# Scan of a hybrid decoder layer: scores and decays placed behind the new state, decays by one minimum and a biased exponential

## The chip, the cores and the metric

One core of one Trainium2 chip. The metric is the device time of one execution of the program in microseconds; it is given as the median of several runs. The engines are TensorE (PE, with its weight loads PEld), VectorE (DVE), ScalarE (ACT), GpSimd (POOL) and SyncE (SP), which here issues the DMA transfers.

## The reference

One decoder layer for a prompt of 1024 tokens and a batch of 8 samples of 4 tokens, width 1024, everything in float32: a SwiGLU block, a mixer, a second SwiGLU block, a gated embedding and a final norm. The change lies in the mixer's chunked scan (16 heads of 64 in 2 groups, state 128, chunks of 128 tokens):

```python
da = dt * a;  xdt = x * dt;  a_cum = cumsum(da)            # within a chunk
seg = a_cum[q] - a_cum[s]
decay_in = where(q >= s, exp(seg), 0)
scores = einsum('qn,sn->qs', C, B)
y_diag = einsum('qs,sp->qp', scores * decay_in, xdt)
decay_out = exp(a_cum[last] - a_cum)
chunk_states = einsum('sn,sp->pn', B, xdt * decay_out)
h = h_prev * exp(a_cum[last]) + chunk_states               # chunk after chunk
y_off = einsum('qn,pn->qp', C, h_prev) * exp(a_cum)
y = y_diag + y_off + d_skip * x
```

## The kernel before, in words

The scan works in 16 units: unit u is chunk u // 2 and head group u % 2 (8 heads). Products of 32-bit precision are made of rounded high and low parts: a tensor is copied to a rounded type on ScalarE (its name ends in h) and the rest is taken on VectorE (its name ends in l); a matmul of two such tensors is three matmuls.

For one unit the functions are called in this order.

- `scan_first` transposes the unit's inputs and B and makes the scores on TensorE, into the banks `btr` and `bsc`. VectorE makes `xd` (x times dt), `skip` writes d_skip times x to `xD`; GpSimd makes `xde`; ScalarE copies B to `bt`. VectorE masks the scores (`sm`) and multiplies the decays `Wa` with them (L1101). Then come parts of the unit before: `scan_lower` gives `wl`, the low part of its weights, and `scan_split` the two parts of its `xD`, `yoh` on ScalarE and `yol` on VectorE. The decays of unit u+1 are loaded by a DMA (`decay_load`, L993) to the half of `Wa` that `scan_lower` has just read for the last time. At the end the parts `xdh` and `xdl` of `xd` are taken.
- One chunk of an independent product (the rest of the input projection, then part of the output projection: 24 matmuls of L258) stands here in TensorE's order, with what the other engines do for it: a weight split now and then (L235, L236) and a copy or an addition of the result (L1214, L1231). In some units pool operands are split as well (L1197, L1198).
- `scan_state` multiplies C with the old state on TensorE; GpSimd decays the state, VectorE scales the result by `eA` to `yo` (written over `xd` here), GpSimd adds it to `xD`; TensorE makes the chunk's state, and VectorE adds it to `h`.
- `scan_last(u - 1)` makes the output of the unit before on TensorE: four groups of five matmuls, in the order yoh, yol, wh by xdh, wh by xdl, wl by xdh (L1158).
- `scan_mid` copies the finished weights of unit u to `wh` on ScalarE and makes the decays of unit u+1 (`decay`): on VectorE eight instructions, one for each head, that subtract a per-partition number from a row of sums and take the minimum with zero (L1000), then one exponential over all eight heads on ScalarE (L1001).
- `y_out(u - 1)` copies the output out of its banks with four copies on ScalarE (L1010) and stores it.
- After an odd unit a second product chunk follows.

The orders of TensorE, VectorE, ScalarE and GpSimd are the order of the program text here (`manual_schedule`); the order of SP's queue is left to the planner. Before the units, `scan_sample` runs for the two groups of the samples; it calls `decay` with 32 tokens. The sums that `decay` subtracts are in `ac`, made once in `steps2`.

Of the kernel before, what the change touches and what calls it, by code (L numbers as in the profile page):

```python
# [10 lines left out]
AF = mybir.ActivationFunctionType  # L11
ALU = mybir.AluOpType
# [3 lines left out]
P = 128  # L16
D = 1024
# [9 lines left out]
GH = 8  # L27
# [29 lines left out]
C_TRI = C_ID + P  # L57
# [26 lines left out]
def emit(tc, dr):  # L84
    nc = tc.nc
    V, S, G, PE, SY = nc.vector, nc.scalar, nc.gpsimd, nc.tensor, nc.sync
# [6 lines left out]
    def new(pool, name, n, dt=F32):  # L93
        uid[0] += 1
        return At(pool.tile([P, n], dt, name=f"{name}_{uid[0]}"))
# [11 lines left out]
    def phase(name, side="left"):  # L107
        return tc.alloc_tile_pool(name=name, bufs=1, side=side, reuse_waits="tile")

    def f(o, n, p0=0, p1=P):  # L110
        return o.f[p0:p1, o.c : o.c + n]

    def r(o, n, p0=0, p1=P):
        return o.t[p0:p1, o.c : o.c + n]

    def cst(o, n, p1=P):
        return f(o_cst + o, n, 0, p1)
# [652 lines left out]
    ph = phase("pooling")  # L770
# [78 lines left out]
    NDT = 9 * H  # L849
    ph_m = phase("mixer", "right")  # L850
    o_bc = new(ph_m, "bc", 4 * T)
    o_dtp, o_ac, o_eA, o_dO = (new(ph_m, f"dt{i}", NDT) for i in range(4))
    o_cd, o_cds = new(ph_m, "cd", P), new(ph_m, "cds", P)
    ph_c = phase("conv", "right")
    o_xb = [new(ph_c, "xb", XCB), new(ph_c, "xb", XCB)]
    o_cv = new(ph_c, "cv", XCB)
# [17 lines left out]
    ph = ph_c  # L874
# [33 lines left out]
    def steps2():  # L908

        da = f(o_e, NDT)  # L910
        PE.matmul(pa[:, 0:128], lhsT=cst(C_TRI, P), rhs=da[:, 0:128], start=True, stop=True)
        PE.matmul(pa[:, 256:384], lhsT=cst(C_ONE, P), rhs=da[:, 0:128], start=True, stop=True)
        PE.matmul(pb[0:S3, 0:H], lhsT=cst(C_TRIS, S3, TS), rhs=da[0:TS, 128:144], start=True, stop=True)
        PE.matmul(pb[0:S3, 32 : 32 + H], lhsT=cst(C_BLK, S3, TS), rhs=da[0:TS, 128:144], start=True, stop=True)
        PE.matmul(pb[:, 128:256], lhsT=cst(C_ONE, P, TS), rhs=f(o_u, NB * H, 0, TS), start=True, stop=True)
        ac, eA, dO = f(o_ac, NDT), f(o_eA, NDT), f(o_dO, NDT)
        G.memset(f(o_ac + 128, H), 0.0)
        G.memset(f(o_dO + 128, H), 0.0)
        V.tensor_copy(ac[:, 0:128], pa[:, 0:128])
        V.tensor_copy(ac[0:S3, 128:144], pb[0:S3, 0:H])  # L920
        V.tensor_tensor(dO[:, 0:128], pa[:, 256:384], ac[:, 0:128], op=ALU.subtract)
        V.tensor_tensor(dO[0:S3, 128:144], pb[0:S3, 32 : 32 + H], ac[0:S3, 128:144], op=ALU.subtract)
        S.activation(eA, ac, AF.Exp)
        S.activation(dO, dO, AF.Exp)
        S.activation(f(o_cd, P), pa[:, 256:384], AF.Exp)
        S.activation(f(o_cds, P), pb[:, 128:256], AF.Exp)
# [12 lines left out]
    for i in range(12):  # L939
# [26 lines left out]
        if i in (0, 2, 3):  # L966
            {0: steps1, 2: steps2, 3: steps3}[i]()
# [8 lines left out]

    ph = phase("scan", "right")
    o_Wa, o_xd, o_xde, o_bt, o_sm = (new(ph, n_, k) for n_, k in (("Wa", 2048), ("xd", 512), ("xde", 512), ("bt", P), ("sm", P)))
    o_h, o_xD2 = new(ph, "h", D), new(ph, "xD", 1024)
    o_xD = o_xD2  # L980
    o_Wh2, o_Wl2 = new(ph, "wh", 2048, F32R), new(ph, "wl", 2048, F32R)
    o_xdh2, o_xdl2 = new(ph, "xdh", 1024, F32R), new(ph, "xdl", 1024, F32R)
    o_yoh, o_yol = new(ph, "yoh", 512, F32R), new(ph, "yol", 512, F32R)
    byd2, btr, bsc, byo, byd = banks[3:8]

    def h3(a):
        return a.rearrange("p (h e) -> p h e", h=GH)

    def by_head(o, hh, nt, k):
        return f(o + hh, GH, 0, nt).unsqueeze(2).to_broadcast([nt, GH, k])  # L990

    def decay_load(o, nt, rows):
        SY.dma_start(h3(f(o, GH * nt, 0, nt)), rows.unsqueeze(0).to_broadcast([nt, GH, nt]))  # L993

    def decay(o, hh, nt):

        ab = f(o, GH * nt, 0, nt)
        ab3 = h3(ab)
        for h in range(GH):
            V.tensor_scalar(ab3[:, h, :], ab3[:, h, :], f(o_ac + hh + h, 1, 0, nt), 0.0, op0=ALU.subtract, op1=ALU.min)  # L1000
        S.activation(ab, ab, AF.Exp)  # L1001

    def y_out(g, t0, nt, yd):

# [8 lines left out]
    def skip(o_y, nt, hh, g):  # L1013

        V.tensor_tensor(h3(f(o_y, 512, 0, nt)), h3(btr[0:nt, :]),
                        vec(V_DSK + GH * g, GH)[0:nt, :].unsqueeze(2).to_broadcast([nt, GH, 64]), op=ALU.mult)
# [65 lines left out]
    def unit(u):  # L1082
        c, g = u // 2, u % 2
        return c, g, c * H + GH * g, c * P

    def scan_first(u):

        c, g, hh, t0 = unit(u)
        B, C = f(o_bc + (g * T + t0), P), f(o_bc + ((2 + g) * T + t0), P)
        for j in range(4):  # L1090
            PE.transpose(btr[:, j * P : j * P + P], f(o_xs + ((4 * g + j) * T + t0), P), ident)
        PE.transpose(bsc[:, 0:P], B, ident)
        PE.matmul(bsc[:, 128:256], lhsT=B, rhs=C, start=True, stop=True)
        bt, sm, xd, xde, ab = f(o_bt, P), f(o_sm, P), f(o_xd, 512), f(o_xde, 512), f(o_Wa + 1024 * (u % 2), 1024)
        ab3 = h3(ab)
        V.tensor_tensor(h3(xd), h3(btr[:, :]), by_head(o_dtp, hh, P, 64), op=ALU.mult)
        G.tensor_tensor(h3(xde), h3(xd), by_head(o_dO, hh, P, 64), op=ALU.mult)
        skip(o_xD2 + 512 * (u % 2), P, hh, g)
        S.copy(bt, bsc[:, 0:P])
        V.tensor_tensor(sm, bsc[:, 128:256], cst(C_TRI, P), op=ALU.mult)  # L1100
        V.tensor_tensor(ab3, ab3, sm.unsqueeze(1).to_broadcast([P, GH, P]), op=ALU.mult)  # L1101
        if u:
            scan_lower(u - 1)
            scan_split(u - 1)
        if u < 15:
            h1 = unit(u + 1)[2]
            decay_load(o_Wa + 1024 * ((u + 1) % 2), P, d_ac[h1 : h1 + GH, :])
        o_xh, o_xl = o_xdh2 + 512 * (u % 2), o_xdl2 + 512 * (u % 2)
        S.copy(r(o_xh, 512), xd)
        V.tensor_tensor(r(o_xl, 512), xd, f(o_xh, 512), op=ALU.subtract)  # L1110

    def scan_state(u):

        c, g, hh, t0 = unit(u)
        C = f(o_bc + ((2 + g) * T + t0), P)
        hg = f(o_h + 512 * g, 512)
        if c > 0:
            yo = f(o_xd, 512)
            PE.matmul(byo[:, :], lhsT=C, rhs=hg, start=True, stop=True)
            G.tensor_tensor(h3(hg), h3(hg), by_head(o_cd, hh, P, 64), op=ALU.mult)  # L1120
            V.tensor_tensor(h3(yo), h3(byo[:, :]), by_head(o_eA, hh, P, 64), op=ALU.mult)
            xD = f(o_xD2 + 512 * (u % 2), 512)
            G.tensor_tensor(xD, xD, yo, op=ALU.add)
        PE.matmul(btr[:, :], lhsT=f(o_bt, P), rhs=f(o_xde, 512), start=True, stop=True)
        if c > 0:
            V.tensor_tensor(hg, hg, btr[:, :], op=ALU.add)
        else:
            V.tensor_copy(hg, btr[:, :])
        if c == 7:
            SY.dma_start(dr["o_ssmp"][:, 512 * g : 512 * g + 512], hg)  # L1130

    def scan_split(u):

        xD = f(o_xD2 + 512 * (u % 2), 512)
        S.copy(r(o_yoh, 512), xD)
        V.tensor_tensor(r(o_yol, 512), xD, f(o_yoh, 512), op=ALU.subtract)

    def scan_mid(u):
        o_W, o_wh, o_wl = (o + 1024 * (u % 2) for o in (o_Wa, o_Wh2, o_Wl2))
        S.copy(r(o_wh, 1024), f(o_W, 1024))  # L1140
        if u < 15:
            decay(o_Wa + 1024 * ((u + 1) % 2), unit(u + 1)[2], P)

    def scan_lower(u):
        o_W, o_wh, o_wl = (o + 1024 * (u % 2) for o in (o_Wa, o_Wh2, o_Wl2))
        V.tensor_tensor(r(o_wl, 1024), f(o_W, 1024), f(o_wh, 1024), op=ALU.subtract)  # L1146
# [13 lines left out]
    def yout_args(u):  # L1160
        return u % 2, u // 2 * P, P, (byd, byd2)

    def scan():
        for g in range(2):
            yield from scan_sample(g)
        decay_load(o_Wa, P, d_ac[0:GH, :])
        decay(o_Wa, 0, P)
        yield
        for u in range(16):
            scan_first(u)  # L1170
            L.get("take", int)()
            yield
            scan_state(u)
            if u:
                scan_last(u - 1)
            scan_mid(u)
            if u:
                y_out(*yout_args(u - 1))
            L.get("take", int)()
            if u % 2:  # L1180
                yield
        scan_lower(15)
        scan_split(15)
        scan_last(15)
        y_out(*yout_args(15))
# [49 lines left out]
    def gated():  # L1235

        for c0, n in CH:
            for m in range(8):
# [11 lines left out]
                yield  # L1250

    a, b = scan(), products()
    done = object()
    with tc.manual_schedule(engines=MS):
# [8 lines left out]
    ph = phase("gated")  # L1263
# [23 lines left out]
    for m in range(8):  # L1287
# [3 lines left out]
        for k in range(4):  # L1291
            h, c, c0, n = k // 2, k % 2, CQ * k, CQ
# [208 lines left out]
```

## Time and profile before

| | us |
|---|---|
| median of 3 runs | 2313.32 (2313.03 to 2315.71) |
| the profiled execution | 2317.03 |
| its span | 2315.2 |
| the sixteen units, from the span's start | about 1074 to 1300 |

The profile is of one execution. PE is the matmuls and PEld their weight loads, which overlap them. In timelines each row is a run of equal instructions: its start, the time from the first start to the last end, engine, line, operation, output and inputs by the program's names, shapes and count; in brackets is the time that the engine sat idle ahead of it and what it waited for. `dt` is the name of the small tables (`ac` and its relatives), `W`, `X` and `tmp` belong to the product chunks. An instruction's record can begin before the record of the one ahead of it on its engine ends, so the distance of two starts is a little shorter than a duration.

### The profile page before, as it was taken

To read this page: it belongs to the slowest core of one execution; us is meant where nothing else is said; L and a number is where in the kernel's file an instruction comes from. 1 tells how busy PE (TensorE), PEld (TensorE's weight loads), DVE (VectorE), ACT (ScalarE), POOL (GpSimd) and SP (SyncE) were. 2 spreads that over 40 slices of the span, in tenths; PEclk is the share of its full clock that TensorE was granted. 3 is DMA by queue.
4 is the path that set the end of the run, shared out by engine and by line. 5 is a ranking of instruction groups with operands and counts; after the bars stand their busy time and mean duration, and the time that the engine had idled before them with its cause. 6 is when DMAs were issued, how large, how long until landed. Compare 5 with 4: busy or idle time off the path is not lost.

```text
span 2315.2 us, 38098 instructions
## 1 busy us (share of the span) xinstructions
PE 2239.8 (97%) x15651; PEld 2186.8 (94%) x15651; DVE 1436.8 (62%) x2113; ACT 791.1 (34%) x1331; POOL 477.2 (21%) x416
## 2 busy tenths in 40 slices
PE   8999999999999999999978989999999999999997
PEld 8999999999999999977867879999999999999997
DVE  7766666654335766555778764576666666334566
ACT  6422222231123114222454543442222233112455
POOL 1112222210003520012222335212222220000333
PEclk9999999999999999999999999999999999999998
DMA  5421222273223333344354654532221227221243
GB/s 182 143 76 68 81 84 79 75 249 105 61 72 100 71 91 68 49 120 149 114 152 144 196 173 135 198 123 79 80 82 66 84 85 262 83 70 51 68 152 131
DMA packets 155711, 257.48 MB, mean 111 GB/s; under 512 B 56784, under 2 KB 101008, under 8 KB 150032
## 3 DMA queue, kind: packets, MB, share of 16 engines
q1 hardware_dynamic: 155536, 255.04, 34.6%
q8 instruction: 123, 2.02, 0.4%
q14 instruction: 52, 0.43, 0.1%
HBM read 195.42 MB, written 59.57 MB: 110 GB/s over the span
## 4 chain that ended last, share of the span: by engine, by line
PE 81%; DVE 7%; DMA 4%; issue 4%; ACT 2%; POOL 1%; SPq 0%; DVEq 0%; ACTq 0%; POOLq 0%
PE bank L258 42%; PE pair L390 31%; PE bank L507 5%; PE bank L1158 1%; DMA Wa<-d_ac 1%; DMA hraw<-d_h 1%; DVE Wa L1000 1%; ACT xs L1010 1%; DVE wl L1146 0%; DMA raw<-wgu 0%; PE bank L1060 0%; PE bank L289 0%; DMA tmp<-d_z 0%; DVE Wa L1101 0%; PE bank L871 0%
## 5 line engine op out<-in xcount | busy, mean ns | idle before, releaser
L258 PE MATMUL bank<-X,W 128*128 128x384 f32 (+1 forms) x4320 | 730.2, 325 | 13.7 <-DVE tmp L1231 4.3
L258 PEld LDWEIGHTS bank<-X,W 128*128 128x128 f32 x4320 | 702.4, 189 | 18.3 <-DVE tmp L1231 4.9
L390 PE MATMUL pair<-X,W 128*128 128x264 f32 x3648 | 458.4, 285 | 0.7 <-DVE cg L417 0.7
L390 PEld LDWEIGHTS pair<-X,W 128*128 128x128 f32 x3648 | 450.8, 188 | 1.0 <-DVE cg L417 1.0
L390 PE MATMUL pair<-E,W 128*128 128x264 f32 x1824 | 235.2, 285 | 0.0
L488 DVE SCALAR_TENSOR_TENSOR x<-bank,x 128x384 f32<-128x384 f32 (+1 forms) x192 | 99.2, 523 | 207.6 <-PE bank L258 203.7
L390 PEld LDWEIGHTS pair<-E,W 128*128 128x128 f32 x1824 | 228.0, 189 | 0.0
L258 PE MATMUL bank<-E,W 128*128 128x384 f32 (+1 forms) x1200 | 217.3, 323 | 0.0
L258 PEld LDWEIGHTS bank<-E,W 128*128 128x128 f32 x1200 | 197.0, 188 | 0.0
L283 POOL TENSOR_TENSOR acc<-acc,tmp 128x384 f32<-128x384 f32 (+2 forms) x89 | 83.0, 932 | 500.7 <-ACT tmp L282 500.6
L379 DVE TENSOR_TENSOR W<-ws,W 128x512 fp32r<-128x512 f32 x152 | 129.9, 855 | 45.9 <-ACT W L378 45.7
L507 PE MATMUL bank<-X,W 128*128 128x264 f32 x1152 | 145.3, 288 | 5.0 <-DVE W L514 2.1
L507 PEld LDWEIGHTS bank<-X,W 128*128 128x128 f32 x1152 | 142.8, 190 | 7.3 <-DVE W L514 2.3
L459 ACT CAST W<-raw 128x640 fp32r<-128x640 f32 (+1 forms) x64 | 49.9, 780 | 252.2 <-PE bank L258 210.9
L420 POOL TENSOR_TENSOR cg<-cg 128x528 f32<-128x528 f32 x38 | 75.1, 1977 | 257.7 <-issue 228.0
L390 PE MATMUL pair<-nd,W 128*128 128x264 f32 x912 | 120.9, 290 | 4.7 <-DVE p L409 4.7
L378 ACT CAST W<-ws 128x512 fp32r<-128x512 f32 x152 | 92.9, 614 | 92.9 <-PE pair L390 85.0
L390 PEld LDWEIGHTS pair<-nd,W 128*128 128x128 f32 x912 | 116.8, 193 | 5.1 <-DVE p L409 5.1
L378 ACT CAST W<-raw 128x512 fp32r<-128x512 f32 x114 | 70.8, 621 | 140.9 <-DMA raw<-wgu 105.3
L258 PE MATMUL bank<-nd,W 128*128 128x384 f32 (+1 forms) x576 | 108.3, 323 | 0.0
L258 PE MATMUL bank<-yh,W 128*128 128x264 f32 x512 | 96.6, 290 | 6.7 <-DVE tmp L1231 6.7
L235 ACT CAST W<-raw 128x1024 fp32r<-128x1024 f32 (+2 forms) x65 | 60.3, 928 | 122.7 <-PE bank L258 109.0
(305 smaller groups left out, 2991.2 us busy)
## 6 DMA issues: line engine op xcount, KB each, us to landing
raw<-wgu SPq DMA_DIRECT2D x43, 1024.0 KB, 4.8
hraw<-d_h SPq DMA_DIRECT2D x44, 528.0 KB, 3.7
d_h<-cg SPq DMA_DIRECT2D x76, 264.0 KB, 2.0
raw<-win SPq DMA_DIRECT2D x28, 512.0 KB, 5.4
raw<-wd SPq DMA_DIRECT2D x32, 384.0 KB, 3.0
raw<-wd SPq DMA_DIRECT2D x32, 320.0 KB, 3.0
Wa<-d_ac SPq DMA_DIRECT2D x16, 512.0 KB, 3.8
raw<-wout SPq DMA_DIRECT2D x16, 512.0 KB, 4.1
```

What stands on the lines that cost most here:

```text
L235: S.copy(r(o_w, n), f(o_r, n))
L258: PE.matmul(ps, lhsT=a, rhs=b, start=i == 0, stop=i == n - 1)
L283: eng.tensor_tensor(f(L["acc"] + c0, n), f(L["acc"] + c0, n), f(o_q, n), op=ALU.add)
L378: S.copy(r(o, 512), f(src, 512))
L379: V.tensor_tensor(r(o + 512, 512), f(src, 512), f(o, 512), op=ALU.subtract)
L390: PE.matmul(ps, lhsT=r(w + (512 * p + P * q), P), rhs=r(x + TH * b, CQ), start=first and q == 0 and j == 0, stop=q == 3 and j == 2, skip_g ...
L420: G.tensor_tensor(f(o_u1, TH), f(o_u1, TH), f(o_g, TH), op=ALU.mult)
L459: S.copy(r(o, n), src)
L488: V.scalar_tensor_tensor(xm, ps, 0.5, xm, op0=ALU.mult, op1=ALU.add)
L507: PE.matmul(ps, lhsT=r(w, P), rhs=r(piece(half(j, h), q) + (TH * b + CQ * c), CQ), start=q + j + i == 0, stop=q == 3 and j == 1 and i == 2)
L1000: V.tensor_scalar(ab3[:, h, :], ab3[:, h, :], f(o_ac + hh + h, 1, 0, nt), 0.0, op0=ALU.subtract, op1=ALU.min)
L1010: S.copy(xs3[q0:q1, 2 * i : 2 * i + 2, :], src)
```

## The change

`scan_first` keeps the transposes, `xd`, `xde`, `skip` and `bt`; `scan_split(u - 1)` and `scan_lower(u - 1)` follow them, in this order. The mask of the scores, the low part of `xd` and the product of scores and decays move to a new function `scan_scores`, called behind `scan_state`. `yo` has a tile of its own. `decay` takes the minimum of the loaded sums and the unit's own sums, all heads in one instruction, and subtracts the own sums as the bias of the exponential, one exponential for each head; the negated sums come from one more instruction in `steps2`.

```diff
--- before.py
+++ after.py
@@ -850,7 +850,7 @@
     ph_m = phase("mixer", "right")
     o_bc = new(ph_m, "bc", 4 * T)
     o_dtp, o_ac, o_eA, o_dO = (new(ph_m, f"dt{i}", NDT) for i in range(4))
-    o_cd, o_cds = new(ph_m, "cd", P), new(ph_m, "cds", P)
+    o_cd, o_cds, o_nac = new(ph_m, "cd", P), new(ph_m, "cds", P), new(ph_m, "nac", NDT)
     ph_c = phase("conv", "right")
     o_xb = [new(ph_c, "xb", XCB), new(ph_c, "xb", XCB)]
     o_cv = new(ph_c, "cv", XCB)
@@ -920,6 +920,7 @@
         V.tensor_copy(ac[0:S3, 128:144], pb[0:S3, 0:H])
         V.tensor_tensor(dO[:, 0:128], pa[:, 256:384], ac[:, 0:128], op=ALU.subtract)
         V.tensor_tensor(dO[0:S3, 128:144], pb[0:S3, 32 : 32 + H], ac[0:S3, 128:144], op=ALU.subtract)
+        V.tensor_scalar(f(o_nac, NDT), ac, -1.0, None, op0=ALU.mult)
         S.activation(eA, ac, AF.Exp)
         S.activation(dO, dO, AF.Exp)
         S.activation(f(o_cd, P), pa[:, 256:384], AF.Exp)
@@ -976,7 +977,7 @@
 
     ph = phase("scan", "right")
     o_Wa, o_xd, o_xde, o_bt, o_sm = (new(ph, n_, k) for n_, k in (("Wa", 2048), ("xd", 512), ("xde", 512), ("bt", P), ("sm", P)))
-    o_h, o_xD2 = new(ph, "h", D), new(ph, "xD", 1024)
+    o_h, o_xD2, o_yo = new(ph, "h", D), new(ph, "xD", 1024), new(ph, "yo", 512)
     o_xD = o_xD2
     o_Wh2, o_Wl2 = new(ph, "wh", 2048, F32R), new(ph, "wl", 2048, F32R)
     o_xdh2, o_xdl2 = new(ph, "xdh", 1024, F32R), new(ph, "xdl", 1024, F32R)
@@ -996,9 +997,9 @@
 
         ab = f(o, GH * nt, 0, nt)
         ab3 = h3(ab)
+        V.tensor_tensor(ab3, ab3, by_head(o_ac, hh, nt, nt), op=ALU.min)
         for h in range(GH):
-            V.tensor_scalar(ab3[:, h, :], ab3[:, h, :], f(o_ac + hh + h, 1, 0, nt), 0.0, op0=ALU.subtract, op1=ALU.min)
-        S.activation(ab, ab, AF.Exp)
+            S.activation(ab3[:, h, :], ab3[:, h, :], AF.Exp, bias=f(o_nac + hh + h, 1, 0, nt))
 
     def y_out(g, t0, nt, yd):
 
@@ -1091,23 +1092,26 @@
             PE.transpose(btr[:, j * P : j * P + P], f(o_xs + ((4 * g + j) * T + t0), P), ident)
         PE.transpose(bsc[:, 0:P], B, ident)
         PE.matmul(bsc[:, 128:256], lhsT=B, rhs=C, start=True, stop=True)
-        bt, sm, xd, xde, ab = f(o_bt, P), f(o_sm, P), f(o_xd, 512), f(o_xde, 512), f(o_Wa + 1024 * (u % 2), 1024)
-        ab3 = h3(ab)
+        bt, xd, xde = f(o_bt, P), f(o_xd, 512), f(o_xde, 512)
         V.tensor_tensor(h3(xd), h3(btr[:, :]), by_head(o_dtp, hh, P, 64), op=ALU.mult)
         G.tensor_tensor(h3(xde), h3(xd), by_head(o_dO, hh, P, 64), op=ALU.mult)
         skip(o_xD2 + 512 * (u % 2), P, hh, g)
         S.copy(bt, bsc[:, 0:P])
-        V.tensor_tensor(sm, bsc[:, 128:256], cst(C_TRI, P), op=ALU.mult)
-        V.tensor_tensor(ab3, ab3, sm.unsqueeze(1).to_broadcast([P, GH, P]), op=ALU.mult)
         if u:
+            scan_split(u - 1)
             scan_lower(u - 1)
-            scan_split(u - 1)
         if u < 15:
             h1 = unit(u + 1)[2]
             decay_load(o_Wa + 1024 * ((u + 1) % 2), P, d_ac[h1 : h1 + GH, :])
+        S.copy(r(o_xdh2 + 512 * (u % 2), 512), xd)
+
+    def scan_scores(u):
+
         o_xh, o_xl = o_xdh2 + 512 * (u % 2), o_xdl2 + 512 * (u % 2)
-        S.copy(r(o_xh, 512), xd)
-        V.tensor_tensor(r(o_xl, 512), xd, f(o_xh, 512), op=ALU.subtract)
+        sm, ab3 = f(o_sm, P), h3(f(o_Wa + 1024 * (u % 2), 1024))
+        V.tensor_tensor(sm, bsc[:, 128:256], cst(C_TRI, P), op=ALU.mult)
+        V.tensor_tensor(r(o_xl, 512), f(o_xd, 512), f(o_xh, 512), op=ALU.subtract)
+        V.tensor_tensor(ab3, ab3, sm.unsqueeze(1).to_broadcast([P, GH, P]), op=ALU.mult)
 
     def scan_state(u):
 
@@ -1115,7 +1119,7 @@
         C = f(o_bc + ((2 + g) * T + t0), P)
         hg = f(o_h + 512 * g, 512)
         if c > 0:
-            yo = f(o_xd, 512)
+            yo = f(o_yo, 512)
             PE.matmul(byo[:, :], lhsT=C, rhs=hg, start=True, stop=True)
             G.tensor_tensor(h3(hg), h3(hg), by_head(o_cd, hh, P, 64), op=ALU.mult)
             V.tensor_tensor(h3(yo), h3(byo[:, :]), by_head(o_eA, hh, P, 64), op=ALU.mult)
@@ -1171,6 +1175,7 @@
             L.get("take", int)()
             yield
             scan_state(u)
+            scan_scores(u)
             if u:
                 scan_last(u - 1)
             scan_mid(u)
```

## Rows read from the trace of the kernel before

**Rows 1.** The page's first part: busy us (share of span) xinstructions

```profile
PE 2239.8 (97%) x15651; PEld 2186.8 (94%) x15651; DVE 1436.8 (62%) x2113; ACT 791.1 (34%) x1331; POOL 477.2 (21%) x416
```

**Rows 2.** Busy time by engine in the scan, clock, DMA share, GB/s

```profile
1074.00:1300.00 226.00, 195.27 (x1159) 174.08 (x1158) 168.35 (x316) 103.11 (x199) 55.34 (x46) 0.96 0.44 135
```

**Rows 3.** Waits in the scan: engine, line, releaser, us in total, times, longest

```profile
PEld bank L1158 <- DVE yol L1136: 23.9, 10, 3.0
...
DVE Wa L1000 <- DMA Wa<-d_ac: 14.7, 9, 7.2
...
DVE sm L1100 <- ACT bt L1099: 10.3, 7, 1.6
```

**Rows 4.** TensorE's timeline, four odd units: start, us, instruction, [idle before <-releaser]

```profile
1095.61 0.39 PE L1158 MATMUL bank<-rii,yol 128*128 128x256 f32 x1
...
1170.87 0.39 PE L1158 MATMUL bank<-rii,yol 128*128 128x256 f32 x1 [2.44 <-DVE yol L1136]
...
1235.92 0.39 PE L1158 MATMUL bank<-rii,yol 128*128 128x256 f32 x1 [0.78 <-DVE yol L1136]
...
1260.13 0.39 PE L1158 MATMUL bank<-rii,yol 128*128 128x256 f32 x1 [2.19 <-DVE yol L1136]
```

**Rows 5.** VectorE's timeline, unit 1's decays, units 13 and 14, and the last wl

```profile
1089.34 1.65 DVE L1000 TENSOR_SCALAR Wa<-Wa,dt 128x128 f32<-128x128 f32 x8
...
1250.78 2.35 DVE L1000 TENSOR_SCALAR Wa<-Wa,dt 128x128 f32<-128x128 f32 x8
1253.05 0.68 DVE L1096 TENSOR_TENSOR xd<-bank,dt 128x512 f32<-128x512 f32 x1
...
1255.94 0.29 DVE L1100 TENSOR_TENSOR sm<-bank,cst 128x128 f32<-128x128 f32 x1 [1.61 <-ACT bt L1099]
1256.27 1.23 DVE L1101 TENSOR_TENSOR Wa<-Wa,sm 128x1024 f32<-128x1024 f32 x1
1257.41 2.07 DVE L1146 TENSOR_TENSOR wl<-Wa,wh 128x1024 fp32r<-128x1024 f32 x1
1259.40 0.68 DVE L1136 TENSOR_TENSOR yol<-xD,yoh 128x512 fp32r<-128x512 f32 x1
...
1260.61 1.21 DVE L236 TENSOR_TENSOR W<-raw,W 128x1024 fp32r<-128x1024 f32 x1
...
1262.21 0.68 DVE L1121 TENSOR_TENSOR xd<-bank,dt 128x512 f32<-128x512 f32 x1
1262.81 0.67 DVE L1126 TENSOR_TENSOR h<-h,bank 128x512 f32<-128x512 f32 x1
...
1291.58 1.22 DVE L1146 TENSOR_TENSOR wl<-Wa,wh 128x1024 fp32r<-128x1024 f32 x1
```

**Rows 6.** ScalarE's timeline, unit 13

```profile
1253.17 1.06 ACT L1001 ACTIVATE Wa<-Wa 128x1024 f32<-128x1024 f32 x1 [5.92 <-DVE Wa L1000]
1254.13 1.49 ACT L1010 COPY xs<-bank 64x256 f32<-64x256 f32 x4
1255.65 0.27 ACT L1099 COPY bt<-bank 128x128 f32<-128x128 f32 x1
1255.81 0.62 ACT L1135 CAST yoh<-xD 128x512 fp32r<-128x512 f32 x1
```

**Rows 7.** GpSimd's timeline, unit 13

```profile
1257.05 1.35 POOL L1120 TENSOR_TENSOR h<-h,cd 128x512 f32<-128x512 f32 x1 [2.19 <-PE bank L1119]
1263.03 1.30 POOL L1123 TENSOR_TENSOR xD<-xD,xd 128x512 f32<-128x512 f32 x1 [4.63 <-DVE xd L1121]
```

**Rows 8.** The page's DMA issues: engine, count, KB each, us to landing

```profile
Wa<-d_ac SPq DMA_DIRECT2D x16, 512.0 KB, 3.8
```

**Rows 9.** ScalarE's groups: count | busy us, mean ns | idle before

```profile
L274 ACT ACTIVATE yh<-tmp,vec 128x384 fp32r<-128x384 f32 x16 | 9.8, 610 | 10.7 <-DVE tmp L1244 8.1 <-DMA d_yf<-xs 2.6
...
L1247 ACT ACTIVATE tmp<-tmp 128x384 f32<-128x384 f32 x14 | 7.1, 509 | 0.0
...
L1001 ACT ACTIVATE Wa<-Wa 32x256 f32<-32x256 f32 x2 | 0.8, 417 | 3.0 <-DVE Wa L1000 3.0
```

## The prediction

> **What bounds the kernel now.** I read the page's busy times first: TensorE is busy for 97% of the span [rows 1], so only a stretch where it waits has something to give, and the one that the diff touches is the scan, from 1074 to 1300 us. The busy times of that stretch come second: 226 us long, 174.08 of them with weight loads, 168.35 with VectorE and 103.11 with ScalarE, so no vector engine is full [rows 2]. Third, the waits in it. The longest of the weight loads is on yol, 23.9 us in ten places; VectorE waits 14.7 for the decay loads and 10.3 for ScalarE's copy bt [rows 3]. The matmuls that wait for yol belong mostly to odd units. From 1095.61 to 1170.87 lie three pairs of units, 25.1 us each; the two pairs to 1235.92 also carry the splitting of pool operands and take 32.5 each; the next takes 24.21 [rows 4]. All numbers below are changes of these periods.
>
> Fourth, why yol is late in an odd unit, by VectorE's and ScalarE's order. Unit 13: eight decay instructions from 1250.78, 2.35 us; the exponential at 1253.17; the four copies of unit 11's output at 1254.13; bt at 1255.65. VectorE has done xd and skip and sits 1.61 us for bt; then sm, the scores' product, wl and yol in a row to 1260.08; TensorE goes on at 1260.13 [rows 4 to 6]. So the pair is set by a loop through two engines, not by either one's load: VectorE has to hand the decays to ScalarE and wait for what stands behind the exponential there.
>
> **The change part by part.** "Step" is from start to start, taken from [rows 5, 6] where no other group is named: yo 0.60 (and so h, xd, yol of the same size), wl and the scores' product 1.14, sm 0.33, the weight split with the tmp that follows it 1.60 (1.13 and 0.47).
>
> Eight subtract-and-min instructions go (2.35 us in unit 13), one minimum of 1024 columns comes. No such minimum is in the trace; the nearest row has the same shape and two inputs in SBUF, 1.22 us with GpSimd quiet and 2.07 beside it [rows 5]. I take 1.22, since GpSimd's add ends before the minimum starts (below). VectorE saves about 1.1 us a unit.
>
> One exponential of 1024 columns goes; its step to the next instruction was 0.96 [rows 6]. Eight of 128 come, with a pointer as bias. bt, 128 columns without pointer, takes 0.27 and the next starts 0.16 later [rows 6]. A pointer operand costs about 0.10: 610 ns with one, 509 without, both 384 columns [rows 9]. So each takes about 0.37. Bounds: 0.16 apart if the pointer hides, 0.37 apart if nothing overlaps; I take 0.29: the full price less the 0.10 or so by which bt overlaps what follows it. Eight steps: 2.32 us (1.28 to 2.96), 1.36 more than before. *The Trainium skill, ScalarE: Activation LUTs, section "What ACT_TABLE_LOAD costs", says that an activation with a pointer bias takes about 280 ns plus 0.833 per column and overlaps its neighbour by 93; an estimate by it is 0.294 a step and 2.35 for eight, and the sum would be the same within a fifth of a microsecond a unit. No run here shows the instruction itself.*
>
> sm, xl and the scores' product move behind the new state. That takes sm off bt's copy. But it puts them between the state and the minimum: the decays of unit u+1 now follow h by 0.33 + xl + 1.14 instead of at once. xl has two SBUF inputs and meets GpSimd's add of yo, which starts 0.82 after yo and runs 1.30 [rows 5, 7]. wl met GpSimd in the same way: it ended 1.08 after GpSimd did, its 1.22 less 0.14 [rows 5, 7]. By that xl (0.68 alone) ends 0.55 after the add, and its step is 1.06 rather than 0.60. What these instructions now cover is the wait for the decay load, which lands 3.8 us after its issue [rows 8] and is still issued behind wl; from the start of wl to the minimum I count 5.34 us below, so most of the 14.7 us goes, except its first wait before unit 0.
>
> The splits of unit u-1 move ahead, to right behind skip. yol reads yoh, and yoh stands in ScalarE's queue behind the decays' exponentials, the four copies and bt. Its cover before was sm, the product and wl, 3.5 us; that cover is gone. This is the new wait. Behind yol stand wl, the issue of the next decay load on SP's queue (it waits for wl), yo and the new state; TensorE's last products wait for yol and wl. xdh still comes after yoh on ScalarE and has slack, since xl reads it only after the state. yo gets its own tile, so the next xd no longer waits for GpSimd's reading of it; xd came later than that anyway, so nothing. The negated sums are one small instruction in the convolution, hidden by matmuls.
>
> **The sum.** One loop, from wl to wl. From even to odd: wl 1.14, tmp 0.47, yo 0.60, h 0.60, sm 0.33, xl 1.06, product 1.14, minimum 1.22: 6.56. Then 0.04 to ScalarE, eight exponentials 2.32, four copies 1.52, bt 0.16, yoh 0.62, 0.02 back: 4.68, while VectorE's xd and skip lie beside it. Then yol 0.60: 11.84. From odd to even the weight split adds 1.13, and GpSimd's decay of the state, which follows the product matmuls, now falls on yol and wl: 0.70. That is 13.67, a pair of 25.5 against 24.2: 1.3 more. In the first three pairs there is no tmp (0.94 less) but a copy of a product ahead of bt in one unit (0.41, a 384-column instruction less its overlap [rows 9]): 25.0 against 25.1, no change.
>
> - three pairs to 1170.87: 0.
> - two pairs to 1235.92: the same exchange, 1.3 each: +2.6.
> - two last pairs: +2.6.
> - start: unit 1's decays come 1.6 later (sm, xl, product and minimum, 3.3 without GpSimd, against 1.65 [rows 5]) and its exponentials 1.36 later, while only yoh, yol and wl (2.6) follow bt where 3.6 did: +2.0.
> - the two sample groups: eight exponentials of 32 columns at 0.18 (bt's step, a pointer more, fewer columns less) are 1.44, against 0.42 less its overlap [rows 9]; the first stands on the chain, the second loses only what VectorE doesn't save: +1.3.
>
> Together +8.5 us. The profiled execution took 2317.03 us (span 2315.2), 3.7 above the median of 2313.32. 2317.03 + 8.5 = 2325.5; less 3.7, 2321.8.
>
> **The rivals.**
> - *The exponentials are cheap.* If each costs the 0.16 step of bt, the loop loses 1.04 in about 14 units, 14.6 us: 2307.2, faster. For it: short ScalarE instructions do overlap [rows 6]; against: the 0.10 of the pointer in every row that has one. *The Trainium skill, Perfetto Trace Analysis, section "Optimizing Scalar/DVE Operations", prices an instruction on ScalarE at a fixed 93 ns only, which stands on this side; the pointer row speaks against it.*
> - *GpSimd isn't met.* If xl and wl run alone, 0.46 twice and 0.70 a pair go, 1.62 in seven pairs, 11.3: 2310.5, the lower edge of no change.
> - *yoh is early enough.* If yoh waits for nothing that is late, yol goes ahead by 3.5 us and the 23.9 us of [rows 3] vanish; with the start's 3.3: 2301. For it only that most even units show no such wait; against: bt was late in seven units, and yoh is behind bt. Faster.
> - *The loads bind.* If the decay load takes 1.3 us longer than its median, the minimum waits about 1.0 in each of seven pairs: 2328.8. It decides from a landing of 4.1 us after wl's end. This is the slower side's far end, together with exponentials that don't overlap (0.64 in 14 units, 9.0: 2330.8).
>
> **How the numbers follow.** Below 0.2%, 4.6 us, this measurement can't tell a change from none. Forecast 0.45, of which 0.05 lies inside no change; loads bind 0.10; exponentials cheap 0.17; GpSimd not met 0.18, of which 0.04 lies in faster; yoh early 0.10. Slower 0.50, within 0.2% 0.19, faster 0.31. The range is from the middle of the cheap cases to just beyond the far end, 2304 to 2332; the forecast's own is 2317 to 2328.
>
> **What would show it.** Right: VectorE's longest wait in the scan is yol for ScalarE's yoh, about 3 us a unit; the eight exponentials start about 0.29 apart; the minimum takes 1.22; the wait for the decay load is nearly gone after unit 0; TensorE waits for wl in odd units and, new, in even ones; the last pairs take about 25.5. Wrong: steps near 0.16, an uncontended xl, or yoh done before skip; any of these and pairs under 24 make it faster.

## The result, and the profile after

The changed kernel is slower: median 2327.4 us of four runs (2324.24 to 2329.55) beside 2313.18 for the kernel before; the ratio is 1.0056, 95% interval 1.0044 to 1.0068, so 10 to 16 us more. The profiled execution took 2329.55 us, 12.5 more than the one of before. The forecast was 2321.8, 8.5 more. Its sign was right; the median lies in the range of 2304 to 2332 and just inside the forecast's own 2317 to 2328, at its slow end. For the profiled execution the prediction's sum gave 2325.5, 4.0 less than it took.

The first part of the page answers [rows 1]: ScalarE has 126 more instructions and 26 us more, VectorE 125 fewer and only 10 us less. The stretch of the scan, the second fence, answers [rows 2]: in the same 226 us TensorE's weight loads lost 7.9 us of busy time, ScalarE gained 18.4 and VectorE lost 14.9. Some of the losses only say that less of the slower scan fits into the same 226 us; ScalarE gained in spite of that. So the engine whose load went down is not the one that sets the end.

```profile
PE 2245.2 (96%) x15651; PEld 2185.6 (94%) x15651; DVE 1426.6 (61%) x1988; ACT 816.8 (35%) x1457; POOL 476.9 (20%) x416
```

```profile
1074.00:1300.00 226.00, 191.19 (x1101) 166.15 (x1100) 153.44 (x198) 121.50 (x301) 53.08 (x46) 0.95 0.41 127
```

The waits of the scan (engine, line, releaser, us in total, times, longest) answer [rows 3]:

```profile
DVE yol L1140 <- ACT yoh L1139: 37.6, 13, 3.6
...
DVE Wa L1000 <- DMA Wa<-d_ac: 11.0, 6, 7.2
PEld bank L1162 <- DVE wl L1150: 10.6, 12, 1.5
...
PEld bank L1128 <- issue: 8.5, 14, 3.2
...
PEld bank L1162 <- DVE yol L1140: 6.1, 12, 1.2
...
PEld bank L1162 <- ACT yoh L1139: 4.4, 9, 2.4
```

VectorE's wait for bt is gone and the one for yoh stands in its place, 2.9 us in each of 13 turns. TensorE's own 23.9 us for yol are cut to 6.1; in their place stand waits for wl (10.6), for yoh (4.4) and for the state's operands (8.5, with no releaser named). TensorE's matmuls with yol, the ones of [rows 4]:

```profile
1097.32 0.38 PE L1162 MATMUL bank<-rii,yol 128*128 128x256 f32 x1
...
1173.83 0.39 PE L1162 MATMUL bank<-rii,yol 128*128 128x256 f32 x1
...
1242.38 0.38 PE L1162 MATMUL bank<-rii,yol 128*128 128x256 f32 x1
...
1267.77 1.23 PE L1128 MATMUL bank<-xde,bt 128*128 128x512 f32 x2 [2.40 <-issue]
1269.02 0.53 PE L1162 MATMUL bank<-rii,yol 128*128 128x256 f32 x1
```

The first three pairs take 76.5 us (75.3 before), the next two 68.6 (65.1), the following one 26.6 (24.2). VectorE from one wl to the next, turns 12 and 13 (start, us, [idle before <- releaser]), answers [rows 5]; ScalarE and GpSimd in the same stretch answer [rows 6, 7]:

```profile
1255.24 2.06 DVE L1150 TENSOR_TENSOR wl<-Wa,wh 128x1024 fp32r<-128x1024 f32 x1
1257.23 0.45 DVE L1236 TENSOR_TENSOR tmp<-bank,tmp 128x288 f32<-128x288 f32 x1
1257.60 0.68 DVE L1125 TENSOR_TENSOR yo<-bank,dt 128x512 f32<-128x512 f32 x1
1258.20 0.67 DVE L1130 TENSOR_TENSOR h<-h,bank 128x512 f32<-128x512 f32 x1
1258.79 0.28 DVE L1112 TENSOR_TENSOR sm<-bank,cst 128x128 f32<-128x128 f32 x1
1258.99 1.26 DVE L1113 TENSOR_TENSOR xdl<-xd,xdh 128x512 fp32r<-128x512 f32 x1
1260.18 1.21 DVE L1114 TENSOR_TENSOR Wa<-Wa,sm 128x1024 f32<-128x1024 f32 x1
1262.29 1.22 DVE L1000 TENSOR_TENSOR Wa<-Wa,dt 128x1024 f32<-128x1024 f32 x1 [0.89 <-DMA Wa<-d_ac]
...
1264.03 0.68 DVE L1016 TENSOR_TENSOR xD<-bank,vec 128x512 f32<-128x512 f32 x1
1268.22 0.69 DVE L1140 TENSOR_TENSOR yol<-xD,yoh 128x512 fp32r<-128x512 f32 x1 [3.51 <-ACT yoh L1139]
1268.83 1.22 DVE L1150 TENSOR_TENSOR wl<-Wa,wh 128x1024 fp32r<-128x1024 f32 x1
```

```profile
1263.54 2.45 ACT L1002 ACTIVATE Wa<-Wa,nac 128x128 f32<-128x128 f32 x8 [1.01 <-DVE Wa L1000]
1265.90 1.48 ACT L1011 COPY xs<-bank 64x256 f32<-64x256 f32 x4
1267.41 0.27 ACT L1099 COPY bt<-bank 128x128 f32<-128x128 f32 x1
1267.57 0.62 ACT L1139 CAST yoh<-xD 128x512 fp32r<-128x512 f32 x1
```

```profile
1254.79 1.43 POOL L1124 TENSOR_TENSOR h<-h,cd 128x512 f32<-128x512 f32 x1 [2.60 <-PE bank L1123]
1258.42 1.29 POOL L1127 TENSOR_TENSOR xD<-xD,yo 128x512 f32<-128x512 f32 x1 [2.19 <-DVE yo L1125]
```

Read them as one loop: the minimum at 1262.29 hands over to the exponentials at 1263.54, these are followed by the copies, bt and yoh, and yoh lets VectorE's yol go at 1268.22. VectorE has done xd and skip by 1264.71 and sits for 3.51 us. TensorE's product of the state reads bt too; it starts at 1267.77, 0.09 us after bt ends, and TensorE had done nothing for 2.40 us.

### The profile page after: what moved, and what is told of

Read it like the earlier page. It is cut to its first block, busy times and chain, and to the rows that moved or that the text cites. A ratio compares the mean times of both kernels' runs of the same rounds, so it can differ in the third digit from the quotient of the medians.

```text
span 2327.7 us, 38065 instructions
## 1 busy us (share of the span) xinstructions
PE 2245.2 (96%) x15651; PEld 2185.6 (94%) x15651; DVE 1426.6 (61%) x1988; ACT 816.8 (35%) x1457; POOL 476.9 (20%) x416
## 4 chain that ended last, share of the span: by engine, by line
PE 40%; DVE 6%; ACT 4%; DMA 3%; issue 2%; POOL 1%; SPq 0%; DVEq 0%; ACTq 0%; POOLq 0%
PE bank L258 20%; PE pair L390 15%; PE bank L507 3%; ACT Wa L1002 1%; DMA Wa<-d_ac 1%; ACT xs L1011 1%; DMA tmp<-d_z 1%; DVE Wa L1000 1%; DVE wl L1150 1%; DMA hraw<-d_h 1%; PE bank L1061 1%; DVE W L236 0%; DVE xdl L1113 0%; DVE Wa L1114 0%; PE bank L289 0%
```

## The experiments

Each was timed beside the kernel before. A time in us is (ratio − 1) × the median of before (2314 to 2315); by that the changed kernel stands at +13.0. Each ratio is uncertain by 2 to 3 us, a difference of two of them by some 4. The theory is that of the prediction: the eight exponentials with their bias lengthen a loop between VectorE and ScalarE, and splitting yol ahead gains little, since yoh stands behind them. The rivals: the moved order is what costs; VectorE's meeting with GpSimd; the loads.

**The two halves of the change, each alone.** The first keeps the changed order and has the old decays:

```
...
-        V.tensor_tensor(ab3, ab3, by_head(o_ac, hh, nt, nt), op=ALU.min)
         for h in range(GH):
-            S.activation(ab3[:, h, :], ab3[:, h, :], AF.Exp, bias=f(o_nac + hh + h, 1, 0, nt))
+            V.tensor_scalar(ab3[:, h, :], ab3[:, h, :], f(o_ac + hh + h, 1, 0, nt), 0.0, op0=ALU.subtract, op1=ALU.min)
+        S.activation(ab, ab, AF.Exp)
```

> The changed order with the decays of the kernel before (eight subtract-and-min instructions, one exponential). Theory, loop through VectorE and ScalarE: the eight exponentials cost 1.4 us a unit on the loop (2.45 against 1.06 in the two profiles) and some 3 us in the two sample groups, so without them about 1.0 a unit in 14 units and the 3 us go: 2313.2 + 14 - 14 - 3, about 2310, between 2306 and 2316; VectorE's wait for yoh shrinks from about 3.5 to about 2 us a unit. Rival, order alone: what costs is that scores and decays stand behind the state and yol behind the output copies, and the exponentials are covered: 2322 or more, with the wait for yoh still above 3 us.

Measured: 0.998 (0.9971 to 0.9989), −4.6 us, as expected, and the wait for yoh falls from 37.6 us to 1.7 a unit:

```profile
DVE yol L1139 <- ACT yoh L1138: 22.3, 13, 2.1
```

The second makes the opposite edit in the kernel before, so the old order with the new decays:

> The order of the kernel before with the new decays (one minimum, eight biased exponentials). Theory: the minimum saves VectorE about 1 us a unit, the exponentials add 1.4 to ScalarE ahead of bt, so the wait of the mask sm for bt grows by 1 to 2 us in odd units, and their loop by 0.3 to 0.5 us; with the sample groups' 3 us: 2317 to 2321. Rival, exponentials alone: the whole 14 us come from them, 2327, whatever the order. Rival, order alone: 2313 or a little less.

Measured: 1.0062 (1.0049 to 1.0076), +14.4 us. Expected was 2317 to 2321, so this missed, upward, and came to the rival's 2327. The wait of the mask for bt was 10.3 us in seven places in the kernel before, and is now:

```profile
DVE sm L1101 <- ACT bt L1100: 22.9, 11, 3.0
```

VectorE and GpSimd show one reason for the miss that I had left out:

```profile
1260.64 1.96 DVE L1000 TENSOR_TENSOR Wa<-Wa,dt 128x1024 f32<-128x1024 f32 x1
...
1266.80 0.29 DVE L1101 TENSOR_TENSOR sm<-bank,cst 128x128 f32<-128x128 f32 x1 [3.00 <-ACT bt L1100]
1267.12 2.03 DVE L1102 TENSOR_TENSOR Wa<-Wa,sm 128x1024 f32<-128x1024 f32 x1
```

```profile
1260.24 1.28 POOL L1124 TENSOR_TENSOR xD<-xD,xd 128x512 f32<-128x512 f32 x1 [2.26 <-DVE xd L1122]
...
1267.03 1.04 POOL L1121 TENSOR_TENSOR h<-h,cd 128x512 f32<-128x512 f32 x1 [2.70 <-PE bank L1120]
```

Right behind the state the minimum meets GpSimd's add and takes 1.96 us; the mask's product meets the state's decay and takes 2.03; the wait for bt is 3.00 where it was 1.61. (Over the sixteen units the minimum takes 1.56 on average.) What this meeting costs by itself was not measured. So it is the decays that cost, and they cost in either order: 14.4 us in the old one and 17.6 in the new (+13.0 against −4.6). The order by itself does not lose.

**Pointer or count?** The changed order with the old decays, and one exponential to each head without a bias:

```
...
-        V.tensor_tensor(ab3, ab3, by_head(o_ac, hh, nt, nt), op=ALU.min)
         for h in range(GH):
-            S.activation(ab3[:, h, :], ab3[:, h, :], AF.Exp, bias=f(o_nac + hh + h, 1, 0, nt))
+            V.tensor_scalar(ab3[:, h, :], ab3[:, h, :], f(o_ac + hh + h, 1, 0, nt), 0.0, op0=ALU.subtract, op1=ALU.min)
+        for h in range(GH):
+            S.activation(ab3[:, h, :], ab3[:, h, :], AF.Exp)
```

> The changed order with the eight subtract-and-min instructions of the kernel before and eight exponentials without a bias, one for each head: it tells the pointer from the number of instructions. If the pointer is what costs (389 ns with it), each takes about 0.29, starts 0.20 apart and can follow its own head's decays, so the last ends about 0.3 after VectorE's: the loop is shorter than with one exponential, 8 to 12 below the kernel before. If eight instructions cost the same without a pointer, or the exponentials wait for all eight decays, 1.6 to 2.4 us follow VectorE: 0 to 10 above the kernel before.

Measured: 0.9977 (0.9967 to 0.9986), −5.3 us; less was gained than expected. ScalarE's group (count | busy us, mean ns) of this kernel, and then of the changed one:

```profile
L1002 ACT ACTIVATE Wa<-Wa 128x128 f32<-128x128 f32 x128 | 27.3, 296 | 5.8 <-DVE Wa L1000 5.6
```

```profile
L1002 ACT ACTIVATE Wa<-Wa,nac 128x128 f32<-128x128 f32 x128 | 39.2, 389 | 9.4 <-DVE Wa L1000 8.9
```

The bias adds 93 ns. Without it the eight go 0.20 apart and take 1.71 us, yet they cost no more than one exponential of 1.06 (−5.3 and −4.6, intervals that overlap). ScalarE's timeline shows why: the eight begin as soon as wh is done, while VectorE's decays (1235.69 to 1237.34) still run.

```profile
1235.86 1.05 ACT L1144 CAST wh<-Wa 128x1024 fp32r<-128x1024 f32 x1 [6.69 <-DVE Wa L1114]
1236.81 1.71 ACT L1002 ACTIVATE Wa<-Wa 128x128 f32<-128x128 f32 x8
1238.42 1.49 ACT L1011 COPY xs<-bank 64x256 f32<-64x256 f32 x4
```

From the product's end (1235.77) to the copies is 2.65 us. In the changed kernel it is 3.53 in a turn in which nothing waits for a load (1235.66 to 1239.19, and the same in the turns at 1248.78 and 1275.36):

```profile
1234.45 1.21 DVE L1114 TENSOR_TENSOR Wa<-Wa,sm 128x1024 f32<-128x1024 f32 x1
```

```profile
1239.19 1.49 ACT L1011 COPY xs<-bank 64x256 f32<-64x256 f32 x4
```

Of this 0.88 a unit, 0.75 is the longer steps (2.36 against 1.61); the other 0.13 is that one minimum for all heads lets no exponential start before it ends. If all 16 units paid it, 0.88 would come to 14.1 of the 18.3 that lie between the two; that is an estimate, and no run keeps the biased exponentials without the one minimum.

**Taking yoh from behind the exponentials.** In the changed kernel yoh is copied one step earlier in ScalarE's order, ahead of wh; then the same with the old decays:

```
-        S.copy(r(o_yoh, 512), xD)
...
+        S.copy(r(o_yoh, 512), f(o_xD2 + 512 * (u % 2), 512))
```

> The changed kernel with one instruction moved: yoh of unit u is taken in front of wh of unit u, so ahead of the exponentials and the output copies on ScalarE, where ScalarE stands idle for the scores' product. Theory: VectorE's wait for yoh (37.6 us in 13 places) is the new wait that sets the loop; it goes, yol and wl follow skip at once, TensorE's waits for yol and wl go with it, and a pair falls from 26 us to TensorE's 22 to 23: 2300 to 2308, below the kernel before. Rival, the wait moves on: bt stands behind the same exponentials and copies, TensorE's state waits for it and the new state with it, and the time stays within 4 us of the changed kernel, 2323 to 2331. Rival, the decay loads bind: VectorE's wait for them, 11.0 us, grows to over 20, 2315 to 2322.

> The changed order with yoh taken ahead of wh and with the decays of the kernel before. Theory: with yoh out of the loop the exponentials no longer set it, so against the run with yoh early and eight exponentials only the sample groups' 3 us are gained, and VectorE's longer decays take some of it back: 2297 to 2306. Rival, the exponentials still bind through bt: 8 us or more below that run.

Measured: 0.9983 (0.9974 to 0.9992), −3.9 us, and 0.9933 (0.9921 to 0.9945), −15.5 us. The first is 17 below the changed kernel, though above the 2300 to 2308 expected: yol waits for yoh nowhere any more, so taking this wait away is worth 17. But the second gains another 11.6 with nothing changed except the decays: the exponentials bind through bt as well, as the rival said. TensorE's load of the state's operand in the first, and ScalarE's bt:

```profile
1253.45 0.30 PEld L1128 LDWEIGHTS bank<-xde,bt 128*128 128x128 f32 x2 [1.25 <-issue]
```

```profile
1253.12 0.27 ACT L1099 COPY bt<-bank 128x128 f32<-128x128 f32 x1
```

The profile names no releaser there; bt ends at 1253.39 and the load starts at 1253.45. In thirteen units of the first kernel the load starts 0.06 to 0.08 us after bt's end; its waits without a named releaser sum to 14.7 us there and to 5.3 in the second. Not all of the 11.6 is bt's: the wait for the decay loads behind the first one shrinks as well, from 3.4 us to 0.8. That the second kernel's 2299.9 lies in the expected 2297 to 2306 is luck, since the theory wanted only some 3 us between the two. It has the lowest ratio of all (the run with the scores alone, below, overlaps it), with pairs of 21 to 23 us at the end, and it beats the kernel before and the changed one.

**wl ahead of yol.** Two calls of the changed kernel exchanged:

```
-            scan_split(u - 1)
             scan_lower(u - 1)
+            scan_split(u - 1)
```

> The changed kernel with two calls exchanged: wl ahead of yol, as in the kernel before; the scores behind the state and the eight biased exponentials stay. Theory, cover: wl (1.14 us) then lies inside VectorE's wait for yoh (3.0 to 3.6 us) instead of behind it, and the loop loses about 1.1 us a unit in 13 to 14 units: 14 to 16 below the changed kernel, so 2 below to 1 above the kernel before; the wait for yoh falls from 37.6 to about 22 us. Rival, the run with the scores alone was fast for the early low part of xd or the single exponential, not for wl's place: 8 above the kernel before or more.

Measured: 1.0006 (0.9997 to 1.0015), +1.4 us, so 11.6 below the changed kernel where 14 to 16 were expected. Its waits for yoh and for the loads:

```profile
DVE yol L1140 <- ACT yoh L1139: 19.4, 12, 2.4
...
DVE Wa L1000 <- DMA Wa<-d_ac: 7.6, 1, 7.6
```

Of 37.6 us half is left, since wl now stands where VectorE idled. The loads, issued behind wl, now go out sooner too, and only the first is waited for; the 11.6 hold both effects. So within the order, the place of yol ahead of wl is the costly step.

**The order's parts, without the new decays.** In the kernel before, first the splits alone ahead of the mask and its product; then the scores alone behind the state, with wl, yol and the operand's split right behind skip, and yo in a tile of its own; then the first with yoh early. The edit of the first, and of the second:

```
-        V.tensor_tensor(sm, bsc[:, 128:256], cst(C_TRI, P), op=ALU.mult)
-        V.tensor_tensor(ab3, ab3, sm.unsqueeze(1).to_broadcast([P, GH, P]), op=ALU.mult)
...
-            scan_lower(u - 1)
             scan_split(u - 1)
+            scan_lower(u - 1)
+        V.tensor_tensor(sm, bsc[:, 128:256], cst(C_TRI, P), op=ALU.mult)
+        V.tensor_tensor(ab3, ab3, sm.unsqueeze(1).to_broadcast([P, GH, P]), op=ALU.mult)
```

```
...
-        V.tensor_tensor(sm, bsc[:, 128:256], cst(C_TRI, P), op=ALU.mult)
-        V.tensor_tensor(ab3, ab3, sm.unsqueeze(1).to_broadcast([P, GH, P]), op=ALU.mult)
...
+    def scan_scores(u):
...
+        V.tensor_tensor(sm, bsc[:, 128:256], cst(C_TRI, P), op=ALU.mult)
+        V.tensor_tensor(ab3, ab3, sm.unsqueeze(1).to_broadcast([P, GH, P]), op=ALU.mult)
...
+            scan_scores(u)
```

> The kernel before with one part of the order alone: the splits of unit u-1 (yol, then wl) ahead of the mask and the scores' product; decays as before. Theory: TensorE's waits for yol in odd units (2.2 to 2.9 us) come from the 3.5 us of VectorE work between skip and yol; moved ahead, yol waits for yoh 0.5 us longer than sm did for bt but comes some 2 us sooner, so most of these waits go and the decays aren't put off: 8 to 13 below the kernel before, a gain larger than that of the whole order (4.6 to 5.7). Rival, the scores have to move as well: 0 to 4 below.

> The kernel before with the other part of the order alone: mask and scores' product behind the new state, with the splits (wl, then yol, then xdl) where they then stand, right behind skip; decays as before, yo in its own tile. Theory: yol comes sooner here too, with wl as the cover for yoh, but the decays come 1.5 us later behind the scores: about as the whole order, 3 to 8 below the kernel before. Rival, the gain of the order lies in the place of yol ahead of wl: no change or slower.

> The splits ahead as in the first of these runs, with yoh taken in front of wh, decays as before, scores where the kernel before has them. If the place of the scores doesn't matter once yoh is out of the loop, this ends where the changed order with yoh early and one exponential ended, 14 to 17 below the kernel before, with pairs of about 21.4 us. If sm's wait for bt still sets odd units, 8 to 12 below.

Measured: 0.9998 (0.9988 to 1.0007), 0.9946 (0.9933 to 0.9958) and 0.9955 (0.9942 to 0.9967): −0.5, −12.5 and −10.4 us. The first missed the 8 to 13 below, as its rival said. yol still waits for yoh, and what is late next is the state: TensorE's transposes wait for h.

```profile
DVE yol L1136 <- ACT yoh L1135: 21.1, 12, 2.1
...
PEld bank L1091 <- DVE h L1126: 12.2, 7, 3.2
```

The second gained more than the 3 to 8 expected, since wl covers yoh's copy. All its waits of yol for yoh:

```profile
DVE yol L1139 <- ACT yoh L1138: 3.6, 6, 1.0
```

The third, 10.4 below, lies in the 8 to 12 of its rival, but not for the rival's reason: sm waits for bt 0.7 us, once. What its trace shows instead is that the transposes still wait for h, 6.2 us, and VectorE for the decay loads, 14.5 us, 8.1 of them for the first.

So the scores behind the state is the step that gains, 12.5 us (yo's own tile is part of this run; in the kernel before no wait of xd for GpSimd shows). The whole order, which splits yol ahead of wl and puts the operand's split between the state and the scores' product, gives 7.9 of them back (−4.6); which of the two does was not told apart with the old decays.

**The smaller terms.** In the changed kernel: a third buffer for the decays, so that a load needn't wait for wl; the old decays in the two sample groups alone; and GpSimd's add of yo left out.

```
...
-            decay_load(o_Wa + 1024 * ((u + 1) % 2), P, d_ac[h1 : h1 + GH, :])
+            decay_load(o_Wa + 1024 * ((u + 1) % 3), P, d_ac[h1 : h1 + GH, :])
...
-            decay(o_Wa + 1024 * ((u + 1) % 2), unit(u + 1)[2], P)
+            decay(o_Wa + 1024 * ((u + 1) % 3), unit(u + 1)[2], P)
```

```
+        if nt == TS:
+            for h in range(GH):
+                V.tensor_scalar(ab3[:, h, :], ab3[:, h, :], f(o_ac + hh + h, 1, 0, nt), 0.0, op0=ALU.subtract, op1=ALU.min)
+            S.activation(ab, ab, AF.Exp)
+            return
```

```
-            G.tensor_tensor(xD, xD, yo, op=ALU.add)
```

> The changed kernel with three buffers for the decays instead of two, so that the load for unit u+1 no longer waits for wl of unit u-1. Theory: the loads take part in the loop in even units only (three waits of about 1.0 us and one of 0.9 in the profile); VectorE's wait for them falls from 11.0 us to the 7.2 ahead of unit 0, and 3 to 5 us go: 9 to 12 above the kernel before. Rival, no part: the yoh wait takes up what the load wait leaves, 13 to 15 above. Rival, the loads are the main cost: 5 or less above.

> The changed kernel with the decays of the kernel before in the two sample groups alone. Theory: sixteen short exponentials there (1.8 us a group against 0.42) cost 2.0 to 2.6 us on the way to the first unit, and what is lost there isn't given back: 10 to 13 above the kernel before. Rival, hidden: 13 to 15 above.

> The changed kernel without GpSimd's addition of yo to the skipped input; the output lacks that term. It prices the meeting of xl and GpSimd (xl 1.26 us in most units, 0.68 alone). Theory: 0.5 to 0.6 us a unit of the loop go in 13 units: 6 to 8 us less than the changed kernel, 6 to 9 above the kernel before. Rival, off the loop: no change, 13 to 15 above.

Measured: 1.0034 (1.0022 to 1.0046), 1.0051 (1.0038 to 1.0064) and 1.0032 (1.0019 to 1.0044), so +7.9, +11.8 and +7.4 us. The third buffer takes away 5 us, the upper end of the 3 to 5 that were expected, and of the wait for loads only the first is left (7.5 us, once). The samples give 1.2, which these intervals can't tell from nothing; how far this stage misses stays open. Without the add 5.6 go, against 6 to 8 expected, while the wait for the loads behind the first one grows from 3.8 us to 8.0. The split of the operand takes what it takes alone; its group in this kernel, then in the changed one:

```profile
L1113 DVE TENSOR_TENSOR xdl<-xd,xdh 128x512 fp32r<-128x512 f32 x16 | 10.9, 679 | 0.0
```

```profile
L1113 DVE TENSOR_TENSOR xdl<-xd,xdh 128x512 fp32r<-128x512 f32 x16 | 18.7, 1170 | 0.0
```

## Why the prediction was right, and where it was short

**The new wait.** Predicted: VectorE's longest wait is yol for yoh, about 3 us a unit. Measured: 37.6 us in 13 places. That this wait costs and isn't only seen is shown from two sides, by yoh early (17 us) and by wl in front (11.6, part of it the loads).

**The exponentials.** Priced 0.29 apart and 0.37 each, 2.32 for eight; measured 0.294, 0.389, and 2.36 from the first to the copies. The 0.29 was in part luck: the prediction's own subtraction, 0.37 less 0.10, gives 0.27, and 2.16 for eight. *The Trainium skill, ScalarE: Activation LUTs, section "What ACT_TABLE_LOAD costs", gives by its formula an estimate of 387 ns for 128 columns and 0.294 us a step; the trace agrees with both (389 ns, 0.294).* The rival that they are cheap is false: it needed steps of 0.16, and with the old decays in their place, one exponential and eight subtractions, the same order takes 17.6 us less.

**GpSimd is met.** The split of the operand was priced at a step of 1.06 and takes 1.19. *The Trainium skill, GPSIMD Engine Reference, section "1. Specifications", says that GpSimd contends with VectorE's instructions that have two inputs in SBUF; the trace agrees, 1170 ns with the add and 679 without.* The rival priced three such meetings in a pair at 11.3 us; only the two with the add were tried, 0.92 a pair or 6.4 in all, and measured 5.6.

**The minimum** takes 1.22 as priced, but only in the new order, where the add has ended; the experiment with the decays alone shows it at up to 1.96.

**One loop, a pair of 25.5.** Two halves were worked out, 11.84 and 13.67. In turns 12 to 13 they measured 13.59 (1255.24 to 1268.83) and then 13.01. The 0.70 for GpSimd's decay of the state, which I had put into the second half, falls into the first (wl 2.06 at 1255.24, 1.22 at 1268.83): no change to the pair. What is really more is 0.89 for the load, a wait of which "most" was to go in the prediction; the remaining 0.2 is in small steps. The pair is 26.6.

**The loads** are thus the step that was too small: the minimum was to come 5.34 us after wl's start and find its data there. wl itself, late by GpSimd, holds the issue back; it ended at 1257.30, and the wait for the load ended at 1262.29, 4.99 later. From a landing of 4.1 the rival decides, and the page's median rose to 4.3 where [rows 8] had 3.8:

```profile
Wa<-d_ac SPq DMA_DIRECT2D x16, 512.0 KB, 4.3
```

The rival had 7 us for it; the trace shows 3.8 behind the first load (11.0 less 7.2), the third buffer 5. So forecast and this rival were both at work.

**The sum by stages**, from the start of the transpose of B in both traces, with 1.18 us added since the samples' first decays began that much earlier after the change than before (1014.74 against 1015.92):

| stage | predicted | measured |
|---|---|---|
| two sample groups (to 1089.97 → 1090.87) | +1.3 | +2.1 |
| start and first three pairs (to 1161.89 → 1165.42) | +2.0 | +2.6 |
| two pairs with pool operands (to 1228.61 → 1235.09) | +2.6 | +3.0 |
| two last pairs (to 1275.61 → 1285.67) | +2.6 | +3.6 |
| end (last yol matmul, 1293.45 → 1305.31) | 0 | +1.8 |

Together +8.5 and +13.0 (the span gained 12.5: 1.18 less for the earlier start, and 0.6 behind the scan). No stage has the wrong sign. Every term was too small, the last two most. The end I had priced at nothing. In the last turn yoh stands behind wh and the four copies, and TensorE waits for it; but the kernel before waited nearly as long there, for yol. After, and then before:

```profile
1304.58 0.38 PE L1162 MATMUL bank<-rii,yoh 128*128 128x256 f32 x1 [2.12 <-ACT yoh L1139]
1305.31 0.39 PE L1162 MATMUL bank<-rii,yol 128*128 128x256 f32 x1 [0.34 <-DVE yol L1140]
```

```profile
1293.45 0.38 PE L1158 MATMUL bank<-rii,yol 128*128 128x256 f32 x1 [2.27 <-DVE yol L1136]
```

From the start of the last product chunk (1298.09, and 1286.70 before) to this matmul are 7.22 us where 6.75 were, so 0.5 of the 1.8. The rest lies ahead of the chunk: the minimum of unit 15's decays waits 1.12 us for its load, and TensorE then 0.51 for wl. So the loads seem to have a part in the end as well; no run tells it apart.

**What the prediction didn't ask**: whether the order alone gains. "yoh early enough" at 2301 was a rival for the whole change, with its new decays. With yoh copied early these gave −3.9 us, about 2309, so the rival's price was too low even where its condition held: bt was left. Only with the old decays as well does the time come below 2301 (2299.9).

## What to carry to other kernels

Where two engines pass work back and forth, cost an edit by what stands behind it in the receiving engine's queue: here 125 instructions fewer on VectorE cost 13 us, because ScalarE's queue to bt and yoh became 1.4 us longer a unit, and to a small part (0.13 a unit) because nothing could start before the one minimum had ended. One instruction that replaces several can lose their hand-over piece by piece, and several with a pointer bias that replace a wide one add up: here 2.36 us for eight against 0.96 for one. Move a consumer ahead only with its producer (yol ahead alone gave −0.5 us, with yoh early −10.4); and run the parts of a change alone, since here one part was worth −12.5 us under a total of +13.

## What the runs showed of the hardware that was not expected

VectorE's instruction with two inputs in SBUF that starts while GpSimd works ends about its own time less 0.14 after GpSimd does, in new places too: the minimum's 1.96 from 1260.64 and the product's 2.03 from 1267.12 end 1.08 after GpSimd's add (1261.52) and decay (1268.07), where alone they take 1.22.

TensorE's clock fell after one of the new waits. The windows of the changed kernel around 1268 (length, busy of PE, PEld, DVE, ACT, POOL, granted clock, DMA share, GB/s):

```profile
1263.00:1268.00 5.00, 2.60 (x12) 1.80 (x11) 1.71 (x3) 4.40 (x14) 2.09 (x2) 1.00 0.15 39
1268.00:1273.00 5.00, 4.88 (x23) 3.84 (x23) 4.78 (x8) 1.65 (x3) 0.61 (x1) 0.66 0.54 151
```

TensorE was busy for 2.60 of the 5 us ahead, and in the next 5 the granted clock averaged 0.66, so part of them at 1.2 GHz instead of 2.4; from 1273 it was 1.00 again. In the kernel before it stays at 1.00 through the last two pairs. The prediction had no term for it. How much of the last pairs' extra microsecond it is was not measured by itself: every version that shortens the wait also moves the work.
